# A two-block transformer layer on one Trainium2 core: the first block's front half rebuilt around the gated-delta-net chain

## The chip, the cores and the metric

The kernel runs on one core of a Trainium2 chip. The metric is the device time of one launch in microseconds (us), the median of the runs. The core's engines are PE (TensorE), DVE (VectorE), ACT (ScalarE), POOL (GpSimd) and SP (SyncE, which here only issues transfers).

## The reference

`reference(x, ...)` sends 256 tokens of width 1024 through two blocks. Block 1, the only one that the change touches:

- `mod = silu(c) @ ada_w + ada_b` gives six rows of 1024 (shift, scale and gate for the mixer and for the feed-forward part); `h = rmsnorm(x) * (1 + scale1) + shift1`; `proj = h @ w_in`.
- **The gated delta net (GDN)**, four heads of 128: a causal convolution over four tokens and silu on queries, keys and values, l2 norms on queries and keys, decays `g` and `beta` from the gates, and then chunk by chunk `t_mat = (I + tril(k_beta k^T * decay, -1))^-1`, `u = t_mat (v beta)`, `o = q state + (q k^T * decay) v_new`, an rmsnorm of `o`, times `silu(z)`.
- **The sparse attention (NSA)**, four heads: compressed keys and values (blocks of 32 tokens through a small MLP), selected blocks and a window; with 256 tokens the last two are full causal attention. Three gates weigh the three outputs.
- `x = x + gate1 * (concat(o_gdn, o_nsa) @ w_out)`, and then a convolved gated feed-forward part.

Block 2 (retention, block attention, product-key experts) follows and is the same in both kernels.

## The kernel before

Activations lie transposed, features on the 128 partitions and the 256 tokens along the free axis; `x` is eight such tiles. Weights come from HBM in chunks of 128x1024 f32 (512 KB) by `Core.weights`: SP issues the transfer into one of four `raw` buffers, ACT rounds the chunk to fp32r (`wh`, L165), and DVE or POOL, by the argument `lo`, computes the residual `wl = raw - wh` (L171). Every projection is then three matmuls, `wh*hH`, `wh*hL` and `wl*hH`, since the activations are split in the same way. A matmul on plain f32 operands shows as two instructions in the trace.

Block 1's mixer (`block1_mix`) goes in these steps:

- **Modulation column by column.** `ada_col` (L220) multiplies one chunk of `ada_w` with `csil` (twice silu of `c`, repeated on all partitions) and sums along the free axis: on DVE in one instruction (L229), or as a product on POOL (L226) and a sum on ACT (L227). `h_of(d)` (L443) needs two such columns for each of the eight tiles of `h`, one on each path; 24 more, in `modulation()` (L926), all on POOL and ACT, are needed only at the block's end.
- **F projection.** The contraction is outermost: with each tile of `h`, one chunk of `w1f` (keys and queries) and one of `w1g` (inputs of the compression, and values), and the gates, are multiplied into PSUM (L453 to L466), 14 accumulators and the gates at once, so that all of PSUM is taken. The last two tiles are done together (`f_tail`).
- **Gates and heads.** `sg` and `gl` are sigmoids and log decays; `conv` (L529), `heads` (L549) and `rstd` (L185, ten small DVE instructions that depend on one another) give keys and queries with their inverse norms; key times key is scaled by columns (`rk`) and by rows (`rows` and `gram`, L611 to L630: PE spreads a column over a row, ACT copies it, DVE or POOL multiplies).
- **The inverse.** The two chunks' 128x128 triangles are inverted by doubling (L668 to L690): at each of six levels PE multiplies, DVE masks (L676), PE multiplies again, DVE subtracts (L689). `tt2` holds the inverse and its transpose side by side, and both are updated.
- **Values and output** (L692 to L743), **NSA** (`nsa()`, L797; `proj1` projects keys, queries and `z` by tokens; `scores` and `values` work head by head, and each head's probabilities are scaled by 1/sum on DVE, L900), and **the output projection** `kouter` with `wo1` (L961), whose results are added to `x` on DVE (L958).

These pieces are Python generators (`gdn`, `nsa`, `modulation`, ...), and the loop over `live` (L940 to L951) interleaves them: until the grams are done one step of each per turn, and then two of `gdn`, one of the others, and one of `modulation` every third turn. The tile framework's scheduler then puts the instructions of each engine into an order of its own, and every engine works in that order.

## Time and profile before

| | |
|---|---|
| median of 3 runs | 1553.77 us (1552.84 to 1556.26) |
| profiled execution, its own time | 1555.88 us |
| its span, first to last instruction | 1554.1 us |
| PE busy in the span | 1487.9 us (96%) |
| DVE, ACT, POOL busy | 1085.2, 727.7, 481.1 us |
| instructions | 27243 |

The profiled execution took 1.8 us more than its span, and 2.1 us more than the median. Views are read by stretches of the span: "start us" counts from the first instruction. A granted clock (PEclk) of 1.00 is TensorE's upper level of 2.4 GHz, 0.50 its lower one of 1.2 GHz, and what lies between is a mean over time.

### The profile page before, as it was taken

Reading aid. Unit: us, or ns where it says so; the run is one execution under the profiler, and the core shown is the slowest. Engines: PE = TensorE matmul, PEld = TensorE weight load, DVE = VectorE, ACT = ScalarE, POOL = GpSimd, SP = SyncE. Lnnn points to the kernel's source line nnn. Section 1 sums busy time; section 2 is a strip of 40 time slices with the busy share of each in tenths; the row PEclk is TensorE's granted clock in tenths of the full one; section 3 lists DMA queues with packets and bytes.
Section 4 is the critical chain, followed back from the end, with each engine's and each line's share of the span. In section 5 each row is a group of like instructions: output and inputs, shape, how many; then the busy total and the mean of one; then the engine's idle time right before and its main releaser. Section 6 shows DMA issues by size and latency. Waiting matters only on the chain.

```text
span 1554.1 us, 27243 instructions
## 1 busy us (share of the span) xinstructions
PE 1487.9 (96%) x10805; PEld 1356.2 (87%) x10805; DVE 1085.2 (70%) x2067; ACT 727.7 (47%) x1077; POOL 481.1 (31%) x265
## 2 busy tenths in 40 slices
PE   5889889999999999999999999999999999999998
PEld 4778779999997788999999999999997877788887
DVE  5885786999766477666399953777768788844443
ACT  3453264666544443644544544444444344444443
POOL 4643771332004450012322222222222222232231
PEclk8998899999999999999999999999999999999999
DMA  7753355466675554357555565555556555556664
GB/s 272 236 164 122 122 167 166 145 189 191 216 260 184 168 165 136 109 175 241 168 152 175 174 191 175 168 171 170 169 170 190 154 172 168 176 176 198 182 185 135
DMA packets 77599, 273.82 MB, mean 176 GB/s; under 512 B 9632, under 2 KB 11296, under 8 KB 76832
## 3 DMA queue, kind: packets, MB, share of 16 engines
q1 hardware_dynamic: 74304, 267.06, 55.3%
q10 hardware_dynamic: 3168, 5.03, 1.0%
q8 instruction: 84, 1.38, 0.4%
q14 instruction: 43, 0.35, 0.1%
HBM read 269.96 MB, written 2.10 MB: 175 GB/s over the span
## 4 chain that ended last, share of the span: by engine, by line
PE 80%; DVE 14%; issue 2%; DMA 2%; ACT 1%; POOL 0%; SPq 0%; DVEq 0%; ACTq 0%; POOLq 0%
PE po L306 8%; PE po L307 8%; PE po L308 8%; PE ps_u L296 6%; PE ps_u L298 6%; PE ps_u L297 6%; PE ps_ko L334 4%; PE ps_ko L333 4%; PE ps_ko L335 4%; DVE wl L171 3%; PE ps_mm L307 2%; PE ps_mm L308 2%; PE ps_mm L306 2%; PE ps_up L297 2%; PE ps_up L298 2%
## 5 line engine op out<-in xcount | busy, mean ns | idle before, releaser
L165 ACT ACTIVATE wh<-raw 128x1024 fp32r<-128x1024 f32 (+1 forms) x446 | 468.8, 1053 | 518.9 <-PE ps_u L297 179.0
L171 POOL TENSOR_TENSOR wl<-raw,wh 128x1024 fp32r<-128x1024 f32 (+1 forms) x143 | 354.4, 2480 | 885.7 <-ACT wh L165 837.3
L171 DVE TENSOR_TENSOR wl<-raw,wh 128x1024 fp32r<-128x1024 f32 x303 | 382.2, 1264 | 174.8 <-ACT wh L165 172.3
L298 PE MATMUL ps_u<-hH,wl 128*128 128x256 f32 x1024 | 287.4, 282 | 6.0 <-DVE wl L171 6.0
L296 PE MATMUL ps_u<-hH,wh 128*128 128x256 f32 x1024 | 292.2, 286 | 0.0
L297 PE MATMUL ps_u<-hL,wh 128*128 128x256 f32 x1024 | 288.7, 282 | 0.4 <-DVE hL L171 0.4
L307 PE MATMUL po<-wl,pH 128*128 128x512 f32 x512 | 203.3, 398 | 0.0
L308 PE MATMUL po<-wh,pL 128*128 128x512 f32 x512 | 201.1, 393 | 0.0
L298 PEld LDWEIGHTS ps_u<-hH,wl 128*128 128x128 f32 x1024 | 193.5, 190 | 7.2 <-DVE wl L171 7.2
L297 PEld LDWEIGHTS ps_u<-hL,wh 128*128 128x128 f32 x1024 | 193.9, 189 | 0.6 <-DVE hL L171 0.6
L296 PEld LDWEIGHTS ps_u<-hH,wh 128*128 128x128 f32 x1024 | 193.1, 189 | 0.0
L306 PE MATMUL po<-wh,pH 128*128 128x512 f32 x512 | 167.7, 400 | 0.5 <-ACT A L1348 0.5
L306 PEld LDWEIGHTS po<-wh,pH 128*128 128x128 f32 x512 | 96.3, 188 | 22.1 <-ACT A L1348 0.6
L307 PEld LDWEIGHTS po<-wl,pH 128*128 128x128 f32 x512 | 96.4, 188 | 22.0
L308 PEld LDWEIGHTS po<-wh,pL 128*128 128x128 f32 x512 | 96.2, 188 | 21.7
L171 DVE TENSOR_TENSOR pL<-A,pH 128x512 fp32r<-128x512 f32 x64 | 64.0, 1000 | 57.1 <-ACT pH L165 57.1
L1438 DVE TENSOR_TENSOR oh<-eq,idx 128x512 f16<-128x512 f16 x64 | 29.4, 459 | 80.7 <-PE ps_G L1444 80.7
L165 ACT ACTIVATE pH<-A 128x512 fp32r<-128x512 f32 x64 | 40.3, 631 | 93.6 <-PE po L307 93.5
L307 PE MATMUL ps_mm<-wl,hH 128*128 128x512 f32 x192 | 77.8, 406 | 1.7 <-DVE wl L171 1.7
L298 PE MATMUL ps_up<-nH,wl 128*128 128x256 f32 x272 | 76.2, 280 | 0.8 <-DVE wl L171 0.8
L308 PE MATMUL ps_mm<-wh,hL 128*128 128x512 f32 x192 | 76.6, 400 | 0.0
L297 PE MATMUL ps_up<-nL,wh 128*128 128x256 f32 x272 | 76.1, 280 | 0.0
(498 smaller groups left out, 3246.3 us busy)
## 6 DMA issues: line engine op xcount, KB each, us to landing
raw<-in_pu SPq DMA_DIRECT2D x128, 512.0 KB, 3.7
raw<-in_pvv SPq DMA_DIRECT2D x128, 512.0 KB, 3.7
raw<-in_up SPq DMA_DIRECT2D x44, 512.0 KB, 3.7
raw<-in_w SPq DMA_DIRECT2D x36, 512.0 KB, 3.7
raw<-in_ada SPq DMA_DIRECT2D x32, 512.0 KB, 3.9
raw<-in_down SPq DMA_DIRECT2D x22, 512.0 KB, 4.5
adaw<-in_ada SPq DMA_DIRECT2D x16, 512.0 KB, 4.6
raw<-in_wo SPq DMA_DIRECT2D x16, 512.0 KB, 4.2
```

The lines of the kernel that those rows point to most:

```text
L165: nc.scalar.activation(H, src, AF.Copy)
L171: eng.tensor_tensor(L, src, H.bitcast(F32), ALU.subtract)
L296: nc.tensor.matmul(ps, wH[:, d], xH[:, d], start=d == 0, stop=False)
L297: nc.tensor.matmul(ps, wH[:, d], xL[:, d], start=False, stop=False)
L298: nc.tensor.matmul(ps, wL[:, d], xH[:, d], start=False, stop=d == KD - 1)
L306: nc.tensor.matmul(ps[t], h, a, start=first, stop=False)
L307: nc.tensor.matmul(ps[t], h, b, start=False, stop=False)
L308: nc.tensor.matmul(ps[t], xL[:, d, t * P:(t + 1) * P], a, start=False, stop=last)
L333: nc.tensor.matmul(o, W[0][:, s], xH[:, r], start=r == order[0] and n % 2 == 0, stop=False, skip_group_check=True)
L334: nc.tensor.matmul(o, W[0][:, s], xL[:, r], start=False, stop=False, skip_group_check=True)
L335: nc.tensor.matmul(o, W[1][:, s], xH[:, r], start=False, stop=r == order[-1], skip_group_check=True)
L1438: nc.vector.tensor_tensor(twos(oh), twos(eq), of(2, t0, n), ALU.mult)
```

## The change

It is all in block 1's mixer; from the output projection's weights on, the code and the engines' orders are those of before (their lines are 42 higher).

- **F** now projects queries, keys and gates only (8 accumulators); the values and the inputs of the compression are projected afterwards, feature tile by feature tile (`fproj`, six chunks of `w1g`, residuals on DVE).
- **Norm of x**: squares on ACT, sums on DVE, one short matmul for each half in place of 16 full ones. The row stays in PSUM.
- **Modulation**: all 16 early columns on DVE with a copy of `csil` in PSUM (`csp`); the 24 later ones on DVE too.
- **POOL** keeps three residuals of F and the masks; all others of the mixer are on DVE.
- **Grams**: the scaling by rows is gone. Key grams are scaled by `rk*rk*beta` by columns, values by the inverse (`irk`), queries' norms go into the last rmsnorm.
- **Inverse**: half the columns in the first product; only `T` is updated, and PE transposes it anew at each level with a copy on ACT. Values and queries are prepared after the second level (`inputs`).
- **Compression**: four partial sums in four 32-column groups of PE (`tile_position`), added by a matmul with `sel`.
- **Scalings** of normed keys and queries, probabilities and outputs on ACT.

```diff
@@ norm, modulation, F
+        csp = psa.tile([P, D], F32, name="csp")
+        nc.vector.scalar_tensor_tensor(csp, k.csil, 1.0, crow, ALU.add, ALU.mult)
+        nc.scalar.activation(k.csil, csp, AF.Copy)
...
-                ada_col(k, 2 * d + s, pl.tile([P, WC], F32, tag="tt", bufs=3, name="adaw"), pool=s == 0)
+                w = pl.tile([P, WC], F32, tag="adaw", bufs=3, name="adaw")
+                nc.sync.dma_start(w, I["ada"][2 * d + s])
+                nc.vector.scalar_tensor_tensor(w, w, 0.5, csp, ALU.mult, ALU.mult,
+                                               accum_out=k.mod[:, 2 * d + s:2 * d + s + 1])
...
             h_of(d)
-            f_rows(d, *F0)
-            f_rows(d, *F1)
+            W = k.weights(I["w1f"][d], lo="pool" if d % 2 and d > 2 else "dve")
+            for n in range(8):
+                f_mm(W, n, d)
...
+        first.close()
+        psp = es.enter_context(tc.tile_pool(name="b1ps", bufs=4, space=PSUM))
@@ grams
-                eng.tensor_tensor(g_[:, h, :T], g_[:, h, :T], rw, ALU.mult)
-                eng.tensor_tensor(g_[:, h, T:], g_[:, h, T:], rw[:, P:], ALU.mult)
...
+        nc.vector.scalar_tensor_tensor(irk, pss, 4.0 * EPS, rk, ALU.add, ALU.mult)
+        nc.vector.tensor_tensor(rk, rk, rk, ALU.mult)
+        nc.vector.tensor_tensor(rk, rk, sg[:, :, 0:4], ALU.mult)
@@ inverse
-                    ps = sp([P, 4, P])
+                    ps = sp([P, 4, 64])
                     for h in range(4):
-                        nc.tensor.matmul(ps[:, h], am[c][:, h], tt2[c][:, 0, h], start=True, stop=True)
-                    m1[c] = g512().rearrange("p (a b) -> p a b", b=P)
-                    nc.vector.tensor_tensor(m1[c], ps, lv[:, lvl, None, :].to_broadcast([P, 4, P]), ALU.mult)
+                        nc.tensor.matmul(ps[:, h], am[c][:, h], half(T_[c][:, h:h + 1], b, 0), start=True, stop=True)
...
+                    if lvl > 1:
+                        ps = sp([P, 4, P])
+                        for h in range(4):
+                            nc.tensor.transpose(ps[:, h], T_[c][:, h], k.ident)
+                        nc.scalar.activation(TT[c], ps, AF.Copy)
@@ projections, compression, probabilities
-            ps = yield from proj_T(k, I["w1t"], c, psm, hH, hL, lo="dve" if c == 1 else "pool")
+            ps = yield from proj_T(k, I["w1t"], c, psm, hH, hL, lo="dve")
...
+        def fproj():
+            for n in range(6):
+                if n % 2 == 0:
+                    ps = nq([P, 2, T])
+                mm_F(k, ps[:, n % 2], k.weights(I["w1g"][n]), hH, hL)
+                if n % 2:
+                    nc.scalar.activation(vr[:, n - 3:n - 1] if n > 1 else kcv, ps, AF.Copy)
+                yield
...
-                        nc.tensor.matmul(pcs[i][:15], X[:, 8 * q + l, :15], rv[:, l], start=q == 0 and l == 0,
-                                         stop=q == 3 and l == 7)
+                        j = 32 * (l % 4)
+                        nc.tensor.matmul(pcs[i][j:j + 16], X[:, 8 * q + l], rv[:, l], start=q == 0 and l < 4,
+                                         stop=q == 3 and l >= 4, tile_position=(0, j), skip_group_check=True)
...
-                        nc.vector.tensor_scalar(prs[t][:, b], prs[t][:, b], s4[:, t, b:b + 1], None, ALU.mult)
+                        nc.scalar.activation(prs[t][:, b], prs[t][:, b], AF.Copy, scale=s4[:, t, b:b + 1])
@@ modulation and the loop
-                ada_col(k, n, pool=True)
+                ada_col(k, n)
...
+        def inputs():
+            yield from fproj()
+            while "level 2" not in done:
+                yield
+            yield from vals()
+            yield from queries()
...
         while live:
-            turn += "grams" in done
             for g in list(live):
-                if g is A and turn:
-                    step(g, 2)
-                elif g is not M or (turn and turn % 3 == 0):
-                    step(g)
+                step(g, 2 if g is B else 1)
```

Three places of the engines' orders. First PE, behind the end of F, in the kernel before (L466 writes F's last accumulators, L558 the sums of squares of the keys' heads, L813 the compression's sums):

```order
L466 MATMUL sp<-hH,wl 128x256
L558 MATMUL sp<-ones,sq 128x1 x2
L813 MATMUL nq<-raw,t_920 15x128 x11
L558 MATMUL sp<-ones,sq 128x1 x2
L813 MATMUL nq<-raw,t_920 15x128 x7
L558 MATMUL sp<-ones,sq 128x1 x2
L813 MATMUL nq<-raw,t_920 15x128 x4
L558 MATMUL sp<-ones,sq 128x1 x2
L813 MATMUL nq<-raw,t_920 15x128 x10
L813 MATMUL nq<-raw,t_963 15x128 x32
```

And in the change, past the middle of `fproj` (L299 to L301; L845 is the compression, L568 the sums of squares):

```order
L299 MATMUL nq<-hH,wh 128x256
L845 MATMUL nq<-raw,t_812 16x128 x6
L568 MATMUL sp<-ones,sq 128x1 x4
L845 MATMUL nq<-raw,t_812 16x128 x2
L300 MATMUL nq<-hL,wh 128x256
L301 MATMUL nq<-hH,wl 128x256
```

The compression stood alone on PE behind F; it now stands in eleven pieces among the 144 matmuls of `fproj`, which were part of F.

Second POOL in the middle of the mixer, before (`am` is the first masked triangle, `qa` the query grams, `raw<-raw,csil` a column of the modulation):

```order
L658 TENSOR_TENSOR am<-ga,lv 128x512 x2
L171 TENSOR_TENSOR wl<-raw,wh 128x1024
L226 TENSOR_TENSOR raw<-raw,csil 128x1024 x3
L171 TENSOR_TENSOR wl<-raw,wh 128x1024 x2
L226 TENSOR_TENSOR raw<-raw,csil 128x1024
L629 TENSOR_TENSOR qa<-qa,rows 128x256
L630 TENSOR_TENSOR qa<-qa,rows 128x128
```

And POOL in the change, from F's third residual to the residuals of the feed-forward part:

```order
L503 TENSOR_SCALAR cneg<-cmask 128x128
L836 TENSOR_TENSOR t_812<-kcv,posT 128x32x15
L836 TENSOR_TENSOR t_993<-kcv,posT 128x32x15
L637 AFFINE_SELECT dec<-dec 128x2x128 x4
L850 MEMSET t_1094 128x128
L860 MEMSET t_1106 128x128
L171 TENSOR_TENSOR wl<-raw,wh 128x1024 x21
```

All work of POOL between the decays' masks and the feed-forward part has moved away.

Third DVE at the fourth and fifth level of the inverse, before (L676 masks, L689 subtracts; the others are NSA's softmax):

```order
L676 TENSOR_TENSOR g_1576<-sp,lv 128x512
L855 TENSOR_TENSOR sc<-nq,cneg 128x128
L857 TENSOR_REDUCE mx<-sc 128x8
L858 TENSOR_TENSOR sc<-sc,mx 128x128
L676 TENSOR_TENSOR g_1589<-sp,lv 128x512
L860 TENSOR_REDUCE mx<-sc 128x8
L689 TENSOR_TENSOR tt<-tt,sp 128x16x16 x2
```

And in the change (L680 masks, L697 subtracts, L232 is a column of the modulation):

```order
L680 TENSOR_TENSOR g_1854<-sp,lv 128x256
L697 TENSOR_TENSOR T<-T,sp 128x16x16
L171 TENSOR_TENSOR wl<-raw,wh 128x1024 x2
L232 SCALAR_TENSOR_TENSOR raw,mod<-raw,csil 128x1024
L171 TENSOR_TENSOR wl<-raw,wh 128x1024
L697 TENSOR_TENSOR T<-T,sp 128x16x16
L232 SCALAR_TENSOR_TENSOR raw,mod<-raw,csil 128x1024
L680 TENSOR_TENSOR g_1941<-sp,lv 128x256
L171 TENSOR_TENSOR wl<-raw,wh 128x1024
L680 TENSOR_TENSOR g_1957<-sp,lv 128x256
```

Between the chain's steps there now stand the wide instructions that were POOL's, and NSA's softmax has moved behind the inverse.

## Rows read from the trace of the kernel before

**Rows 1.** Stretches of the span by stage: busy time of each engine, granted clock, DMA
```profile
0.00:26.05 26.05, 7.04 (x36) 6.59 (x36) 14.15 (x26) 8.58 (x13) 11.91 (x17) 0.84 0.83 294
26.05:82.50 56.45, 48.49 (x363) 46.13 (x364) 47.50 (x69) 27.27 (x49) 32.63 (x18) 0.92 0.69 222
82.50:125.33 42.83, 37.88 (x265) 32.29 (x264) 34.49 (x98) 21.32 (x52) 15.71 (x14) 1.00 0.53 163
125.33:241.06 115.73, 103.07 (x593) 91.68 (x592) 82.27 (x167) 53.69 (x137) 70.40 (x36) 0.84 0.45 146
241.06:264.10 23.04, 23.04 (x195) 22.74 (x194) 14.81 (x32) 9.33 (x11) 1.75 (x1) 1.00 0.52 161
264.10:1554.10 1290.00, 1268.41 (x9362) 1156.79 (x9360) 891.98 (x1679) 607.50 (x818) 348.67 (x181) 1.00 0.57 175
```

**Rows 2.** Timeline of DVE: start, duration, line, operation, tiles, what ended a wait
```profile
9.17 1.23 DVE L397 SCALAR_TENSOR_TENSOR csil<-csil,crow 128x1024 f32<-128x1024 f32 x1 [9.17 <-ACT csil L371]
...
52.59 3.42 DVE L171 TENSOR_TENSOR wl<-raw,wh 128x1024 fp32r<-128x1024 f32 x1
...
61.57 1.22 DVE L229 SCALAR_TENSOR_TENSOR adaw<-adaw,csil 128x1024 f32<-128x1024 f32 x1
...
63.10 0.16 DVE L448 TENSOR_TENSOR md<-md,c_norms 128x1 f32<-128x1 f32 x1
63.28 1.23 DVE L171 TENSOR_TENSOR wl<-raw,wh 128x1024 fp32r<-128x1024 f32 x1
...
264.10 1.69 DVE L958 SCALAR_TENSOR_TENSOR x<-ps_ko,mod,x 128x256 f32<-128x256 f32 x4 [3.40 <-PE ps_ko L335]
```

**Rows 3.** Timeline of POOL in the same stretch of F
```profile
52.34 2.59 POOL L226 TENSOR_TENSOR adaw<-adaw,csil 128x1024 f32<-128x1024 f32 x1
54.89 2.81 POOL L171 TENSOR_TENSOR wl<-raw,wh 128x768 fp32r<-128x768 f32 x1
```

**Rows 4.** DVE by line and shape, 125 to 241 us: busy us, mean ns, idle before
```profile
L900 DVE TENSOR_SCALAR pr<-pr,s 128x256 f32<-128x256 f32 x8 | 8.7, 1128 | 0.1
L689 DVE TENSOR_TENSOR tt<-tt,sp 128x256 f32<-128x256 f32 x22 | 8.2, 412 | 6.2 <-PE sp L686 6.1
L676 DVE TENSOR_TENSOR g<-sp,lv 128x512 f32<-128x512 f32 x12 | 8.2, 682 | 0.8 <-PE sp L674 0.7
```

**Rows 5.** POOL by line and shape, 73 to 262 us
```profile
L226 POOL TENSOR_TENSOR raw<-raw,csil 128x1024 f32<-128x1024 f32 x24 | 56.6, 2373 | 23.8 <-DMA raw<-in_ada 13.2 <-DVE tt L663 6.2 <-ACT pr L890 3.0
```

**Rows 6.** Timeline of PE at F's end, twelve matmuls in a row: first and last
```profile
76.00 0.28 PE L464 MATMUL ps_f<-hH,wh 128*128 128x256 f32 x1
...
77.29 0.28 PE L464 MATMUL sp<-hH,wh 128*128 128x256 f32 x1
```

**Rows 7.** PE by line and shape, 82.5 to 125.3 us
```profile
L813 PE MATMUL nq<-raw,t 128*15 128x128 f32 x128 | 14.7, 273 | 0.1
```

**Rows 8.** Timeline of PE: one product of the inverse, and one tiled product
```profile
170.21 1.92 PE L674 MATMUL sp<-tt,ga 128*128 128x128 f32 x8
...
186.59 1.11 PE L674 MATMUL sp<-tt,ga 128*128 128x128 f32 x8
...
206.84 0.48 PE L910 MATMUL nq<-pcT,vcm 16*128 16x128 f32 x2
207.25 1.16 PE L914 MATMUL nq<-pT,vv 128*128 128x128 f32 x8
```

**Rows 9.** Two more stretches: busy DVE is the third engine's number
```profile
180.00:220.00 40.00, 38.62 (x254) 33.34 (x254) 33.93 (x73) 22.74 (x60) 33.22 (x15) 1.00 0.54 182
...
280.00:330.00 50.00, 46.53 (x383) 45.69 (x382) 48.89 (x84) 34.57 (x73) 18.97 (x8) 1.00 0.53 159
```

**Rows 10.** Waits, 0 to 320 us: total us, number, longest
```profile
POOL raw L226 <- DMA raw<-in_ada: 13.2, 6, 9.4
```

**Rows 11.** DMA issues: number, KB each, us to landing
```profile
raw<-in_ada SPq DMA_DIRECT2D x32, 512.0 KB, 3.9
```

**Rows 12.** ACT by line and shape, 125 to 241 us
```profile
L227 ACT ACTIVATE raw<-raw 128x1024 f32<-128x1024 f32 x24 | 25.1, 1046 | 2.1 <-POOL raw L226 2.1
```

More of the change, by code (lines that the diff above doesn't have):

```diff
@@ L225, in ada_col @@
     if pool:
-        nc.gpsimd.tensor_tensor(raw, raw, k.csil, ALU.mult)
+        for q in range(0, WC, WC // pool):
+            v = raw[:, q:q + WC // pool]
+            nc.gpsimd.tensor_tensor(v, v, k.csil[:, q:q + WC // pool], ALU.mult)
         nc.scalar.activation(raw, raw, AF.Copy, scale=0.5, accum_out=k.mod[:, n:n + 1])
@@ L379, in block1_mix @@
         psm = es.enter_context(tc.tile_pool(name="b1pm", bufs=4, space=PSUM))
-        psp = es.enter_context(tc.tile_pool(name="b1ps", bufs=4, space=PSUM))
+        first = es.enter_context(ExitStack())
+        psa = first.enter_context(tc.tile_pool(name="b1pa", bufs=1, space=PSUM))
         k.sm = sm
@@ L583, in block1_mix @@
         pv = k.c1["pv"]
+        gq1 = pl.tile([P, 1], F32, name="gq1")
+        nc.vector.tensor_scalar(gq1, pv[:, 1:2], P ** -0.5, None, ALU.mult)
         def g512():
@@ L687, in gdn @@
-                    for i in both:
-                        tv = half(tt[:, i], b, i)
-                        nc.vector.tensor_tensor(tv, tv, ps[:, i].rearrange("p h (n b) -> p h n b", b=b), ALU.subtract)
+                            nc.tensor.matmul(ps[:, h], TT[c][:, h], m1[c][:, h], start=True, stop=True)
+                        else:
+                            nc.tensor.matmul(ps[:64, h], m1[c][:, h], TT[c][:, h, 64:], start=True, stop=True)
+                    if lvl < 6:
+                        tv = half(T_[c], b, 0)
+                        nc.vector.tensor_tensor(tv, tv, ps.rearrange(split, b=b), ALU.subtract)
+                    else:
+                        tv = TT[c][:64, :, 64:]
+                        nc.vector.tensor_tensor(tv, tv, ps[:64], ALU.subtract)
@@ L763, in proj1 @@
             for t in range(NT):
-                nc.vector.tensor_tensor(raw[t][:, :n], pr[t][:, :n], r[:, t, :, None].to_broadcast([P, n, P]), ALU.mult)
+                for i in range(n):
+                    nc.scalar.activation(raw[t][:, i], pr[t][:, i], AF.Copy, scale=r[:, t, i:i + 1])
             for i in range(n):
@@ L800, in nsa @@
             vcm = pl.tile([P, P], F32, name="vcm")
+            sel = pl.tile([P, 16], F32, name="sel")
+            nc.vector.tensor_reduce(sel, k.ident.rearrange("p (a b) -> p b a", b=32)[:, :16], AX.X, ALU.add)
             pcs = []
@@ L842, in nsa @@
             yield from proj1(1)
-            live.extend((gate(), vals()))
-            mix.append(pl.tile([P, KD, T], F32R, tag="yk", name="mH"))
+            live.append(gate())
+            mix.append(pl.tile([P, KD, T], F32R, name="mH"))
             mix.append(pl.tile([P, KD, T], F32R, name="mL"))
@@ L853, in nsa @@
             nc.gpsimd.memset(pc, 0.0)
[L854 removed]
+            sc = low.rearrange("p (t h n) -> p t h n", t=NT, h=4)
             nc.vector.tensor_tensor(sc, psc, cneg, ALU.add)
```

211 lines of the change are left out of this document (106 added, 105 removed).

## The prediction

> **What bounds the kernel now.** I read the busy time by stretches first [rows 1]. Only block 1's mixer differs, and the engines' orders are the same from the output projection on; so the reader should cut the span where the first result of that projection is added to `x`, at 264.10 us [rows 2]. The 1290.0 us behind it, in which PE is busy 1268.4, are taken over unchanged. The forecast is the time at which this addition starts in the new kernel, and nothing else.
>
> Ahead of it there are five stretches: 26 us until F begins, 56.5 us of F, 42.8 us to the inverse, 115.7 us of inverse, projections and attention, and 23.0 us of output projection [rows 1]. PE is never the full bound there: it is idle 8 us in F, 5 in the third stretch, 12.7 in the fourth, and the granted clock is 0.92 and 0.84 in F and the fourth, a mix of the two levels (2.4 and 1.2 GHz) with PE's idle gaps ahead of the lower one. One product of the inverse takes 1.11 us where the clock is up and 1.92 where it is down [rows 8].
>
> Next, what the gaps wait for. A residual on DVE takes 1.23 us alone and 3.42 us when POOL works through two products beside it [rows 2, 3]; instructions with two operands in SBUF come to a standstill there. A DVE instruction that reads PSUM doesn't: L676 kept 682 ns, L689 412 ns, over a stretch in which POOL was busy 70.4 of 115.7 us, whereas the scaling L900 took 1128 ns for the same 256 elements [rows 1, 4]. So POOL's help lengthens DVE's chain, and DVE's chain is what PE waits for.
>
> **The change, part by part.**
>
> *Start.* The product with `c` starts at 9.17 us [rows 2]; it hangs on the same transfer and the same ACT instruction as before, so I keep it. The norm's 16 matmuls go; two short ones and ACT squares replace them, and the first matmul of F still needs the same row, so nothing is gained before 26 us. The sums of squares are in the DVE count that follows.
>
> *F.* DVE's order, from that product to the last tile of `h`, holds 16 column sums (1.22 us each: 19.5), 6 residuals (1.2: 7.2), one other 1024-wide instruction (1.2), 3 of 512 (0.68: 2.0), 17 of 256 (0.41: 7.0), 3 of 128 (0.3, an estimate between 0.41 and 0.16: 0.9) and 28 small ones (0.16: 4.5) [rows 2, 4]: 42.3 us, so 51.5. POOL keeps three residuals. The column sums read `csp` in PSUM, which lets them pass; the others can be held by up to 2.4 us each time, 0 to 7.2 in all. I take half, 3.6. Behind the last tile, ACT's rounding (0.5) and the 48 matmuls of the last two tiles at 0.117 us (12 of them start within 1.29 us [rows 6]) make 6.1. **F ends at 61.2 us** instead of 82.5. Transfers: 24 chunks of 512 KB replace 24 plus 8 smaller ones; before, 222 to 294 GB/s were moved [rows 1], and 12.6 MB at 294 take 43 us; they begin ahead of DVE's 42.3 us of work, which hides them. I cost them at nothing; at 222 they take 57 us and would end F some 9 us later, which stays in the range.
>
> *To the inverse.* Now PE is the bound. `fproj` is 144 matmuls of 0.117: 16.8. The compression's 128 instructions took 14.7 us [rows 7]. It is tiled in the change, and its price isn't in the trace: the only tiled product there, L910, needed 0.41 us for two instructions until the next began [rows 8], no quicker than plain ones. Bounds: a quarter of 14.7 plus 0.2 for each of eleven visits (5.9), and 14.7 plus the same 2.2 (16.9). I take 14.7, the value nearest L910. What else PE did in the third stretch: 37.9 busy, less 14.7, less 48 matmuls of 512 columns that now come later (twice 0.117 each: 11.2), less 16 instructions for spreading rows that vanish (1.8): 10.2 stays. Masking the triangles, now two 512-wide DVE instructions: 1.4. Together 43.1: **the inverse starts at 104.3 us** (before: 125.3). DVE has 31 us of work in this time and keeps up; ACT loses POOL's column sums and has room.
>
> The Trainium skill, "TensorEngine Tiling (Array Packing)", section Key Properties, says that different tiles load and multiply in parallel, but also that changing the tiling mode drains TensorE. By its first half the compression would take 5.9 us and the forecast would be 9 us lower; by its second half and L910, it is the 14.7 to 16.9 above. The rival below carries it.
>
> *Inverse to output projection.* Here DVE gets what POOL had: 22 of the 24 column sums fall here. On POOL they took 56.6 us [rows 5]. DVE's order from the masking to the last head's residual holds 22 sums (26.8), 14 residuals ahead of the output projection's last five (16.8), 13 instructions of 512 (8.8), 55 of 256 (22.6), 26 of 128 (7.8) and 95 small ones (15.2): 98.0 us. PE has about as much (three token projections 33.7, the inverse 232 instructions at 0.14 or less [rows 8], the attention, all at the upper clock) and fits beside it; ACT loses the 24 sums (25.1 [rows 12]) and gets 16 probability scalings and some 40 shorter copies in their stead. So DVE is the bound, and the question is how dense it runs. In the busiest 40 us of the old stage, with the clock up, it was busy 33.93 (85%), with POOL beside it; at the start of the feed-forward part 48.89 of 50 (98%) [rows 9]. I take 90%, nearer the first since the chain is the same: 109 us, from 102.9 to **211.8**.
>
> *Output projection.* Until the first addition it needs 156 matmuls (18.3 us) and the last head's remainder, some 2: before, the stretch was 23.04 with more of the attention in it [rows 1]. **The first addition starts at 232.3 us.**
>
> *Sum.* 264.1 - 232.3 = 31.8 us gained: 21.3 in F, nothing more to the inverse (it now contains `fproj`), 10.5 after it. The profiled execution took 1555.88 us, 2.1 more than the median shown, 1553.77; the same gain on the median gives **1522 us**.
>
> **Rivals.**
>
> *The tiled compression runs its column groups side by side.* For: the four groups write disjoint partitions, and the 64 products are ordered group after group. Against: L910, and eleven switches between tiled and plain products. It lies on PE's path to the inverse, so 14.7 becomes 5.9: **1513 us**. Chance 0.22.
>
> *DVE waits as much as before.* In the old fourth stretch it was busy 82.27 of 115.73, 71% [rows 1]. The inverse's steps depend on one another through PE, and in the new order wide instructions stand between its masks and subtractions; each may hold the next step by 1.2 us. Against: part of those waits came from POOL, and values, queries and projections now fill PE. 98.0 at 71% is 138 us instead of 109: 29 of the 31.8 us are gone, **1551 us**. Chance 0.13.
>
> *Slower: DVE stands still for transfers.* All chunks share four `raw` buffers and one queue in order. POOL waited 13.2 us, six times, for columns of `ada_w` [rows 10], and nobody cared; DVE now takes them in order with the chain behind it. A landing takes 3.9 us [rows 11]. If 8 of the 24 sums wait for a whole landing (31.8/3.9), the gain is gone; if half of them do, 47 us are lost: **1569 us**. For: one such wait on POOL lasted 9.4 us. Against: only six in 24 waited, and the queue moved 146 GB/s where 294 have been seen. Chance 0.05.
>
> *The clock.* If PE has more gaps in the inverse, its 232 instructions cost up to 24 us more at the lower level (0.81 us for eight [rows 8]), as they partly did before; this is inside the second rival's price and gets no chance of its own.
>
> *The change doesn't take POOL out of the chain.* The order speaks against it: behind F, POOL has only masks and the windows' additions. What remains beside DVE, three residuals in F, is priced. Chance 0.02, at about no change.
>
> **How the numbers follow.** The forecast has 0.58. Its own range: 98% instead of 90% on DVE is 9 us less and no collision in F another 3.6 less (1509); 80% is 13.5 more, full collision 3.6, late transfers 9 (1548, if all come together). Adding the compression at its quick end and the nearer half of the 71% case, **1505 to 1546** leaves about 0.08 below and 0.12 above. A difference of 0.2% (3 us) is what a measurement of this kernel can tell. Faster: 0.58 + 0.22 and most of the second rival's 0.13, 0.92; the same: the rest of it, the last rival and a little of the third, 0.04; slower: 0.04.
>
> **What would show it.** In the new profile: F's last matmul near 61 us; residuals on DVE at 1.2 us throughout, and none above 2 behind F; the first masked triangle at 103, the inverse at 104; DVE busy about 90% from there to 212 with column sums between the level's steps; the first addition near 232 us; and 1290 us behind it. The tiled compression shows itself at once: 64 products in 6 or in 15 us of PE's time. I am wrong on the first step if F ends past 66 or before 57; on the third if DVE is busy under 80% or the chain's longest waits name a transfer; and on everything if what lies behind the first addition changes by more than 3 us.

## The result and the profile after

The changed kernel is 1.0% slower: 1567.78 us median (six runs, 1566.32 to 1573.1) against 1553.3 us for the kernel before (six runs); the ratio is 1.010, 95% interval 1.0076 to 1.0123. The forecast was 1522 us, and its range ended at 1546. The profiled execution took 1567.32 us with a span of 1565.6 us, so the same cut as before the change can be made, at the first addition to `x`.

Stretches of the span of the changed kernel (length, busy time and count of PE, PEld, DVE, ACT, POOL, granted clock, DMA share, GB/s). In order: up to F's first matmul; F; from F's end to the inverse's first product; the inverse; from the first masked triangle to the last head's residual (99.91 to 256.90, for which the prediction took 109 us); what lies behind the first addition; 20 us around the start of the inverse; and everything from F's end to the first addition:

```profile
0.00:28.10 28.10, 2.18 (x8) 1.86 (x8) 16.34 (x41) 9.79 (x15) 2.90 (x17) 1.00 0.92 329
28.10:63.05 34.95, 29.62 (x217) 28.16 (x218) 27.62 (x51) 12.25 (x19) 8.55 (x8) 0.95 0.71 241
63.05:108.54 45.49, 36.14 (x342) 30.98 (x343) 38.41 (x100) 23.55 (x54) 5.38 (x8) 0.88 0.65 209
108.54:190.69 82.15, 73.80 (x385) 65.61 (x385) 52.09 (x131) 24.42 (x64) 0.00 (x0) 0.75 0.52 164
99.91:256.90 156.99, 130.72 (x632) 110.78 (x633) 87.68 (x249) 58.56 (x156) 0.20 (x1) 0.73 0.39 125
...
276.69:1565.60 1288.91, 1266.51 (x9362) 1154.88 (x9360) 891.21 (x1679) 606.96 (x818) 348.94 (x181) 1.00 0.57 175
100.00:120.00 20.00, 10.93 (x45) 9.59 (x46) 18.20 (x44) 5.70 (x14) 0.20 (x1) 0.50 0.56 163
63.05:276.69 213.64, 183.74 (x1123) 159.62 (x1124) 123.51 (x337) 86.02 (x212) 7.25 (x9) 0.79 0.44 141
```

Against [rows 1]: behind the first addition nothing changed (1288.91 us for 1290.0). F ends at 63.05 instead of 82.5, so 19.5 us are gained there. Then all of it is lost, and more: from F's end to the first addition the changed kernel takes 213.64 us, where the kernel before takes 181.5.

The same stretch in the kernel before:

```profile
82.60:264.10 181.50, 163.90 (x1048) 146.61 (x1047) 131.48 (x295) 84.24 (x198) 87.76 (x51) 0.90 0.48 152
```

Of the 32.1 us, PE's busy time is 19.8 (183.74 less 163.90) and its idle time 12.3 (29.9 less 17.6). The instruction counts differ by 7%, but busy time multiplied by granted clock is nearly the same: 183.74 x 0.79 is 145, 163.90 x 0.90 is 148. So PE did about as much, longer, at a lower mean clock. In the runs below that product comes to 143 to 149, once 139 (the two with extra matmuls left aside), which makes this reading a rough yardstick: what a version loses is PE's idle time, plus PE's busy time above some 146 us.

Where it begins is in the timeline of PE of the changed kernel, from the end of the compression on (start, duration, line, operation, tiles, what ended the idle time before):

```profile
95.88 0.40 PE L854 MATMUL nq<-sel,t 128*128 128x16 f32 x2
100.65 2.11 PE L662 MATMUL sp<-ident,am 128*128 128x128 f32 x8 [4.37 <-DVE am L659]
105.21 0.80 PE L863 MATMUL nq<-c,t 128*128 128x128 f32 x2 [2.45 <-DVE t L861]
108.54 3.68 PE L677 MATMUL sp<-T,ga 128*128 128x64 f32 x16 [2.53 <-DVE T L665]
114.18 3.68 PE L692 MATMUL sp<-g,TT 128*128 128x64 f32 x16 [1.96 <-DVE g L680]
119.33 1.97 PE L677 MATMUL sp<-T,ga 128*128 128x64 f32 x8 [1.47 <-DVE T L697]
...
129.70 0.47 PE L309 MATMUL ps_mm<-wh,hH 128*128 128x512 f32 x1
```

From 96 to 125 us PE has only the chain and the compression's small network (L854, L863), and it waits for DVE at nearly each step; the granted clock of 100 to 120 us is 0.50, which is the lower of its two levels (1.2 of 2.4 GHz). The first matmul of the token projections, the wide work that doesn't hang on the chain, comes at 129.70. What DVE does meanwhile is in its timeline:

```profile
117.65 1.23 DVE L232 SCALAR_TENSOR_TENSOR raw<-raw,csil 128x1024 f32<-128x1024 f32 x1 [1.73 <-DMA raw<-in_ada]
...
118.87 0.40 DVE L697 TENSOR_TENSOR T<-T,sp 128x256 f32<-128x256 f32 x1
...
119.64 0.40 DVE L697 TENSOR_TENSOR T<-T,sp 128x256 f32<-128x256 f32 x1
...
121.33 0.43 DVE L680 TENSOR_TENSOR g<-sp,lv 128x256 f32<-128x256 f32 x1 [0.49 <-PE sp L677]
```

A column sum (L232) waits 1.73 us for its transfer, takes 1.23, and only then come the subtractions (L697) for which PE's product at 119.33 waited. All column sums and all residuals of weights in the stretch from F's end to the first addition, by line and shape (busy us, mean ns, idle before):

```profile
L171 DVE TENSOR_TENSOR wl<-raw,wh 128x1024 fp32r<-128x1024 f32 x25 | 30.4, 1221 | 33.7 <-ACT wh L165 33.5
L232 DVE SCALAR_TENSOR_TENSOR raw<-raw,csil 128x1024 f32<-128x1024 f32 x24 | 29.4, 1226 | 15.8 <-DMA raw<-in_ada 13.2 <-PE sp L634 2.4
```

Residuals and sums run at their undisturbed 1.22 us: POOL is out of the way, as meant. But 18 of the 24 sums stand between the inverse's steps (22.0 us inside 108.54 to 190.69).

### The profile page after: what moved, and what is told of

Same layout as the page of the kernel before. It is cut to its first block, busy times and chain, and to the rows that moved or that the text cites. A ratio compares the mean times of both kernels' runs of the same rounds, so it can differ in the third digit from the quotient of the medians.

```text
span 1565.6 us, 26969 instructions
## 1 busy us (share of the span) xinstructions
PE 1482.0 (95%) x10707; PEld 1344.5 (86%) x10707; DVE 1058.7 (68%) x2105; ACT 715.0 (46%) x1062; POOL 367.6 (23%) x214
## 4 chain that ended last, share of the span: by engine, by line
PE 77%; DVE 15%; DMA 4%; issue 2%; ACT 2%; ACTq 0%; DVEq 0%
PE po L309 8%; PE po L310 8%; PE po L311 8%; PE ps_u L299 7%; PE ps_u L301 6%; PE ps_u L300 6%; PE ps_ko L337 4%; PE ps_ko L336 4%; PE ps_ko L338 4%; DVE wl L171 4%; DMA raw<-in_ada 2%; PE ps_mm L310 2%; PE ps_mm L309 2%; PE ps_mm L311 2%; PE ps_G L1485 1%
## 5 line engine op out<-in xcount | busy, mean ns | idle before, releaser
L165 ACT ACTIVATE wh<-raw 128x1024 fp32r<-128x1024 f32 x444 | 468.6, 1057 | 515.4 <-PE ps_u L300 181.8
L171 POOL TENSOR_TENSOR wl<-raw,wh 128x1024 fp32r<-128x1024 f32 x130 | 325.7, 2507 | 996.8 <-ACT wh L165 945.1
L171 DVE TENSOR_TENSOR wl<-raw,wh 128x1024 fp32r<-128x1024 f32 x314 | 391.2, 1248 | 197.6 <-ACT wh L165 196.2
L301 PE MATMUL ps_u<-hH,wl 128*128 128x256 f32 x1024 | 287.5, 282 | 6.0 <-DVE wl L171 6.0
L299 PE MATMUL ps_u<-hH,wh 128*128 128x256 f32 x1024 | 292.1, 286 | 0.0
L311 PE MATMUL po<-wh,pL 128*128 128x512 f32 x512 | 201.1, 393 | 0.0
L301 PEld LDWEIGHTS ps_u<-hH,wl 128*128 128x128 f32 x1024 | 193.5, 190 | 7.2 <-DVE wl L171 7.2
L299 PEld LDWEIGHTS ps_u<-hH,wh 128*128 128x128 f32 x1024 | 193.1, 189 | 0.0
L309 PE MATMUL po<-wh,pH 128*128 128x512 f32 x512 | 167.7, 400 | 0.5 <-ACT A L1390 0.5
L309 PEld LDWEIGHTS po<-wh,pH 128*128 128x128 f32 x512 | 96.3, 188 | 22.2 <-ACT A L1390 0.6
L311 PEld LDWEIGHTS po<-wh,pL 128*128 128x128 f32 x512 | 96.2, 188 | 21.7
L301 PE MATMUL ps_up<-nH,wl 128*128 128x256 f32 x272 | 76.0, 280 | 0.8 <-DVE wl L171 0.8
L311 PE MATMUL ps_mm<-wh,hL 128*128 128x512 f32 x192 | 76.7, 401 | 0.0
L299 PE MATMUL ps_up<-nH,wh 128*128 128x256 f32 x272 | 75.8, 279 | 0.0
```

What stands on the lines that cost most here:

```text
L165: nc.scalar.activation(H, src, AF.Copy)
L171: eng.tensor_tensor(L, src, H.bitcast(F32), ALU.subtract)
L299: nc.tensor.matmul(ps, wH[:, d], xH[:, d], start=d == 0, stop=False)
L301: nc.tensor.matmul(ps, wL[:, d], xH[:, d], start=False, stop=d == KD - 1)
L309: nc.tensor.matmul(ps[t], h, a, start=first, stop=False)
L311: nc.tensor.matmul(ps[t], xL[:, d, t * P:(t + 1) * P], a, start=False, stop=last)
```

## The experiments

The theories, by the letters in the expectations. On the 24 sums: **A** and **T**, late transfers of the columns in DVE's order; **B** and **D**, the sums' own DVE time (DVE is the bound; in e18's expectation D is worded as S is here); **C**, they use DVE's idle time and the loss is elsewhere; **Q**, their place in the one queue, ahead of the projections' weights; **R**, a column in the shared buffers costs wherever it stands; **S**, sums between the inverse's levels delay the chain. On PE: **K**, its gaps keep it at the lower level; **P**, its independent work comes too late behind the compression's network. Each stretch quoted below is F's end to the first addition, columns as above; the scheduler reorders other instructions with each edit, so whole orders are compared.

### What do the 24 columns cost?

e1 takes them out (columns 16 to 39 of `mod` become zeros):

```
-   ada_col(k, n)
+   if n == 16: nc.gpsimd.memset(k.mod[:, 16:40], 0.0)
```

> The changed kernel without the 24 later modulation columns: neither their transfers nor their sums (the 24 values are set to 0, so gate, shift and scale of the output projection and the feed-forward part are wrong). Theory A (DVE stands still in its order for columns that land late): the first addition to x comes at 235 to 245 us instead of 276.7, the time is 1526 to 1536 us. Theory B (the sums' own 29 us stand in DVE's order ahead of the inverse's steps): the same, 1530 to 1540. Theory C (the sums lie in DVE's idle time; the attention comes last, one head after the other, behind the inverse): within 6 us of the changed kernel, 1562 to 1568.

e2 keeps the sums and drops the transfers (sums over `csil`, so those columns are wrong values):

```
-   ada_col(k, n)
+   w = pl.tile([P, WC], F32, tag="adaw", bufs=3, name="adaw")
+   nc.vector.scalar_tensor_tensor(w, k.csil, 0.5, k.csil, ALU.mult, ALU.mult, accum_out=k.mod[:, n:n+1])
```

> The changed kernel with its 24 later column sums on DVE, but taken over a tile that lies in SBUF all the time (csil twice), so that the columns' transfers are left out and the values are wrong. Theory A (late transfers): nearly all of what the kernel without sums gains, 1528 to 1540 us, and DVE dense between the inverse's steps. Theory B (the sums' own time): no more than the 13.2 us of direct waits for columns come back, 1553 to 1562. Theory C: 1562 to 1568, as without sums.

e3 gives the columns the three `adaw` buffers instead of the shared ones; e4 keeps the shared ones but gives the columns back to POOL and ACT:

```
+   e3: ada_col(k, n, pl.tile([P, WC], F32, tag="adaw", bufs=3, name="adaw"))
+   e4: ada_col(k, n, pool=1)
```

> The changed kernel with three buffers of their own for the 24 later columns (those of the early columns, idle by then) instead of the four that they share with the weights. Theory A in the form that the shared buffers hold the transfers up: DVE's waits for columns (13.2 us, 10 times) and ACT's for weights shrink to under 5 us, and the time falls by 8 to 20 us, to 1548 to 1560. If the one queue in order and the landing time of 4 to 5 us decide, not the buffers: less than 4 us of difference. Theories B and C: less than 4 us too.

> The changed kernel with the 24 later columns where they were before: the product on POOL, the sum on ACT. Theory A and B: DVE's order is free of them, nothing in the chain waits for a column; some DVE instructions with two SBUF operands stand still beside POOL (24 products of 2.4 us, each holding one of them up by 1 to 2 us where they meet, 10 to 20 us in all), so 1540 to 1555 us. Theory C: no change from moving them, but the collisions come on top, 1565 to 1580.

Measured: e1 1526.54 us (0.982 of before, 0.977 to 0.988), e2 1542.89 (0.993, 0.990 to 0.996), e3 1535.62 (0.990, 0.984 to 0.995), e4 1563.38 (1.007, 1.004 to 1.010). Without the columns the change is worth 27 us; with them it costs 14, so the columns cost 41 us. C falls, and e1 can't tell A from B. e2, e3 and e4 lie outside every range that was named for them, and e2 and e3 don't say why the columns are dear, since the order moved: in e2 sums went into F (which ended at 73.6), in e3 all 24 stood ahead of the inverse, whose first product came at 138.7. Both are nevertheless quicker than the change. In e4 DVE's 29.4 us of sums are gone, yet it is as busy (125.7 us), because other instructions were stretched beside POOL's products. DVE by line and shape of e4 shows it:

```profile
L545 DVE SCALAR_TENSOR_TENSOR t<-yk,gconv,t 128x253 f32<-128x253 f32 x4 | 3.8, 976 | 0.0
L545 DVE SCALAR_TENSOR_TENSOR t<-vr,gconv,t 128x253 f32<-128x253 f32 x4 | 3.6, 913 | 0.0
...
L923 DVE TENSOR_SCALAR m<-m 128x4 f32<-128x4 f32 x4 | 3.3, 834 | 0.1
```

The first of them takes 470 ns in the changed kernel, the second 472, the third 164. The Trainium skill, "SBUF — State Buffer", section "Who interferes with whom", says that a DVE instruction with two SBUF inputs contends with a GpSimd instruction that reads SBUF; the two rows of L545 agree. They are the smaller part, though: most of the stretching fell on small instructions of the dependent chains (the steps of `rstd`, the softmax), some of which, as L923, have one tensor operand.

### Is it the pace, the queue or the buffers?

e5 steps the columns in every third turn after the grams; e10 makes one ring of seven buffers; e14 issues all 24 ahead of the loop; e11 is the kernel before with a column in every turn:

```
+   e5:  turn += "grams" in done
+        if g is not M or (turn and turn % 3 == 0): step(g, 2 if g is B else 1)
+   e10: tag="raw", bufs=7 (columns, weights and the early columns)
+   e14: step(M, 6)                  # in each of the four turns ahead of the loop
+   e11: (turn and turn % 3 == 0)  ->  turn      # in the kernel before
```

> The changed kernel, shared buffers, with a later column only every third turn and only once the key grams are done, as in the kernel before; nothing else. On the queue 8 of the 12 chunks of the token projections' weights then stand ahead of all columns but one, and the last 2 behind 4 columns instead of 14. Theory Q (on the one queue with its four shared buffers the columns stand ahead of the token projections' weights, so the attention's inputs come late): the first addition at 240 to 255 us, the time 1530 to 1545. Theory R (a column in the shared buffers costs the same wherever it stands in the queue): 1555 to 1568. Theory S (the gain with buffers of their own came from the sums standing ahead of the inverse in DVE's order): 1560 or more, since they don't here.

> The changed kernel with one ring of seven shared buffers in place of four shared and three for the early columns. Same memory, same order of code. Theory Q in the form that buffers decide (a column that waits to be summed keeps a buffer from the weights): about what own buffers gave, 1530 to 1545. Theory Q in the form that the place in the queue decides: the columns still stand ahead of the weights, 1555 to 1566. Theory S: 1560 or more, since most sums still stand between the inverse's levels.

> The changed kernel, shared buffers, sums on DVE, all 24 later columns taken ahead of the inverse (six in each of the four turns before the loop); nothing else. Theory S (sums and their waits between the inverse's levels cost the time, not the buffers): DVE does them in one stretch, PE idles once and then runs the inverse and the attention closely packed at the upper clock, as with own buffers: the first addition at 240 to 252 us, 1530 to 1545 us. Theory Q or R (buffers or place in the queue): the weights of values and of the compression now stand behind 18 to 24 columns, which is the worst case: 1570 or more.

> The kernel before with a later column on every turn once the grams are done instead of every third; the sums stay on POOL and ACT. On the queue the last 4 of the 12 chunks for the token projections stand behind 7 to 10 columns instead of 2 to 4. Theory Q: slower than the kernel before by 5 to 20 us. Theories R and S: within 4 us of the kernel before, as the columns, their buffers and DVE's order of sums are the same.

Measured: e5 1562.16 us (1.007, 1.004 to 1.009), e10 1563.68 (1.007, 1.004 to 1.010), e14 1561.56 (1.008, 1.005 to 1.011), e11 1548.54 (0.999, 0.997 to 1.001). Pace and the number of buffers are worth 4 to 6 us of the 41 (e5, e10). e11 speaks against Q: the kernel before took 1551.0 us beside it, and no loss came. e14 met no forecast: S had 1530 to 1545 us for it, Q and R 1570 or more. In it 20 sums stand ahead of the inverse's first product (117.7), and it gains little; a likely reason is in SP's timeline (start, duration, line, tiles, number of issues):

```profile
105.73 9.34 SPq L225 DMA_DIRECT2D raw<-in_ada  x6
116.48 6.56 SPq L840 DMA_DIRECT2D raw<-in_cv  x4
123.18 51.05 SPq L158 DMA_DIRECT2D raw<-in_w1t  x12
```

The projections' weights are issued only behind the columns, from 123.18 on, in the same four buffers; in the changed kernel the first is issued at 93.16. So with shared buffers the sums can be early or the weights can, not both.

### Sums ahead of the chain, or between its steps

What differs by intent is the place. All have the convolutions of values held behind the inverse's second level. e7 gives the columns their own buffers; although the program steps them from level 1 on, the scheduler takes most of them ahead of the inverse, since nothing holds them; e9 also lets each transfer start only behind a subtraction of the inverse, so all 24 sums stand between its steps; e18 is e9 with the sums over `csil`, without transfers; e8 holds the convolutions alone, in the change's shared buffers.

```
+   nc.vector.scalar_tensor_tensor(gv, held[0][:, 0, :32], 0.0, gv, ALU.mult, ALU.add)   # all four: hold
+   ada_col(k, n, <adaw tile>); M stepped from "level 1" on                              # e7
+   nc.vector.tensor_copy(mk, T_[c][:, 0, :1])      # e9, e18: mark behind a subtraction
+   nc.gpsimd.tensor_copy(w[:, :1], marks[-1])      # e9, e18: ahead of each column
```

> The changed kernel with own buffers for the columns, and the convolutions of values and queries not before the second level (their coefficients are written anew from a result of the first). Most of the sums stand ahead of the inverse, 15 us of convolutions between its levels. Theory S: the inverse's first product 10 to 15 us earlier than at 138.7 with own buffers alone, and since the convolutions need no transfer the chain behind it is only a little slower: 1522 to 1536. Theory D or K in the form that any wide work between the levels opens PE's gaps: most of the gain is lost again, 1545 to 1562.

> The changed kernel with shared buffers and sums as they are, but the convolutions of values and queries not before the inverse's second level. Theory P: 15 us of DVE's work leave the place ahead of the compression's network, the projections start 8 to 15 us earlier than 129.7 and the time falls by 5 to 20 us, 1546 to 1561. Theory D: the wide work between the levels grows, 1565 to 1580.

> The changed kernel with the columns' own three buffers, but each column's transfer may start only after a step of the inverse (a mark that DVE writes behind the subtractions), so that the sums stand between the levels; the convolutions of values and queries can't start before the second level either (their coefficients are written anew from a result of the first). Theory Q: the weights pass the columns, so no slower than with own buffers alone, and the inverse's first product comes at 95 to 105 us instead of 138.7 there: 1515 to 1535. Theory S: with the sums between the levels again, the chain is as slow as in the changed kernel: 1550 to 1568.

> The kernel with gated columns (own buffers, sums between the inverse's levels, convolutions held), but each sum taken over csil twice, which lies in SBUF: the 24 columns' transfers are left out, and the values are wrong. In the kernel with the transfers DVE waited 8.2 us for columns. Theory T (waits for the transfers in DVE's order make the place between the levels dear): 1524 to 1540 us, near the kernel with the sums ahead of the inverse (1523.9). Theory D (1.2 us of DVE between two dependent steps is dear by itself, wherever the data lie): 1548 to 1560, no more than the 8.2 us back.

Measured: e7 **1523.87 us** (0.982, 0.978 to 0.986), e8 1568.17 (1.010, 1.007 to 1.013), e9 1559.36 (1.004, 1.002 to 1.006), e18 1560.56 (1.006, 1.003 to 1.008). The stretch in e7, then its part ahead of the inverse, the inverse, and the rest:

```profile
65.74:232.02 166.28, 154.58 (x1123) 136.67 (x1124) 121.63 (x331) 85.16 (x212) 10.00 (x9) 0.95 0.47 164
65.74:119.63 53.89, 46.81 (x394) 40.41 (x395) 52.13 (x124) 23.70 (x51) 8.14 (x8) 0.97 0.90 323
119.63:184.38 64.75, 60.21 (x391) 53.21 (x390) 45.04 (x144) 35.60 (x107) 0.00 (x0) 0.89 0.23 78
184.38:232.02 47.64, 47.56 (x342) 43.05 (x341) 24.46 (x65) 25.85 (x55) 1.86 (x1) 1.00 0.32 100
```

The same stretch, the inverse and the rest in e9:

```profile
63.63:263.76 200.13, 175.93 (x1123) 154.57 (x1124) 124.49 (x347) 86.57 (x212) 14.26 (x33) 0.84 0.46 150
97.72:185.47 87.75, 72.41 (x381) 65.06 (x382) 72.50 (x185) 33.12 (x83) 7.96 (x26) 0.77 0.68 228
185.47:263.76 78.29, 70.05 (x404) 59.87 (x404) 28.83 (x96) 37.28 (x94) 1.86 (x1) 0.85 0.19 61
```

DVE by line and shape, the sums ahead of the inverse in e7:

```profile
L232 DVE SCALAR_TENSOR_TENSOR adaw<-adaw,csil 128x1024 f32<-128x1024 f32 x18 | 23.0, 1283 | 0.5 <-DMA adaw<-in_ada 0.4
```

And the sums inside the inverse in e9:

```profile
L232 DVE SCALAR_TENSOR_TENSOR adaw<-adaw,csil 128x1024 f32<-128x1024 f32 x24 | 29.3, 1220 | 8.3 <-DMA adaw<-in_ada 8.2
```

DVE has about the same work in both (121.63 and 124.49 us), and so has PE by the yardstick above (147 and 148). e7 starts its inverse 22 us later, with DVE at 97% ahead of it, and yet has its inverse done at 184.38 where e9 needs until 185.47. So the chain isn't done later in e9; what is lost lies behind it. There PE has 47.6 us left in e7, at the full clock and without a gap, for e9's 78.3 us. Of these 30.7 us, 8.2 are idle time of PE, 10.5 the lower clock and 11.9 more work left over (70.05 x 0.85 is 59.5, against 47.6), the projections among it: 30 matmuls of L309 to L311 for 48. The idle time is nearly all attention, whose products wait for ACT's probabilities, as e9's waits from 185.47 to 263.76 say (total us, number, longest):

```profile
PE nq L946 <- ACT pr L942: 7.9, 2, 4.2
```

The place, with what the scheduler moves along with it, is worth 35 us by the medians. In the two profiled executions 31.7 us of their difference lie ahead of the first addition and 7.0 behind it, where the code is the same. And e18, where the 24 transfers are gone, is no quicker than e9:

```profile
63.20:271.04 207.84, 174.88 (x1124) 152.05 (x1124) 123.50 (x347) 86.52 (x212) 23.54 (x33) 0.83 0.27 84
```

So A, T, Q and R fall as the main cause, and so do B and D as an amount of work, since DVE's work is equal. S stands as far as the place goes; how it delays the rest is more than the chain alone, as the 30.7 us show. Two reservations: e9 and e18 carry small marks and POOL copies that e7 doesn't, and e18's DVE waited 12.6 us for ACT's rounding of weights instead of e9's 2.4, so "transfers cost nothing" holds for the total, not for each wait. e8 shows that holding the convolutions does nothing while the sums stay where they were.

### Is it PE's clock, or its order?

e12 fills PE's gaps in the change with 224 unread matmuls of 256 columns (26.2 us at the 0.117 us of F's end [rows 6]); e13 does it in e9:

```
+   fill(ps, n): n x nc.tensor.matmul(ps[:, 256:], hH[:, 0, :P], hH[:, 0, :T], start=True, stop=True)
+   24 ahead of each of two first transposes, 6 per product, 8 per head
```

> The changed kernel with matmuls that nobody reads put into PE's order where it waits: 24 of 256 columns ahead of each of the two first transposes, 6 ahead of each product of the inverse, 8 ahead of each head's output, 224 in all, 26 us at the upper clock. Theory K (the gaps cost little by themselves, but keep PE at its lower clock, where the same work takes 33 us longer): the granted clock between 111 and 257 us rises from 0.75 to 0.9 or more, and the time falls to 1540 to 1558 in spite of the added work. Theory D (DVE's order is the bound, and PE's clock only follows): the clock rises too, but the time stays within 5 us of 1566 or grows by up to 20.

> The same 224 unread matmuls in the kernel with gated columns (own buffers, sums and convolutions between the levels). Theory K: faster than without them, 1530 to 1550 instead of 1559. Theory D: 1555 to 1580.

Measured: e12 1566.92 us (1.012, 1.006 to 1.018), e13 1570.67 (1.013, 1.008 to 1.017). The stretch in e12:

```profile
64.47:272.83 208.36, 192.73 (x1348) 173.19 (x1348) 123.76 (x336) 85.93 (x212) 7.48 (x9) 0.91 0.45 144
```

The clock rose from 0.79 to 0.91. If the filler is taken at its 26.2 us (an estimate), PE's other busy time is 166.5 us instead of 183.7, and its idle time 15.6 instead of 29.9: 31.5 us gained, 26.2 paid for the filler; nothing measurable in the kernel's time is left. Both times lie in D's ranges and outside K's, and e13 is 11 us slower than e9. So the part of K that filled gaps raise the granted clock is shown; that the clock by itself sets the time is not.

e15 puts the first token projection ahead of the compression's network; e17 does it in e7:

```
+   nc.scalar.activation(pcT[j:j + 16, i], pcs[i][j:j + 16], AF.Copy)   # both banks copied at once
+   yield from proj1(0)
    for i, n in enumerate("kv"):
...
-   yield from proj1(0)
    yield from proj1(1)
```

> The changed kernel, its columns, buffers and convolutions as they are; only the first token projection (16 of the 48 passes of three matmuls, and the transposes behind it) stands ahead of the compression's small network instead of behind it (the compression's four partial sums are copied to SBUF at once, so their PSUM banks come free). Theory P (PE's independent work comes too late: it waits for the compression's small network, whose DVE steps stand among sums, residuals and convolutions, so PE is idle ahead of the inverse, has gaps in it, and does the last projection and the attention behind it): the projection starts at 97 to 103 us instead of 129.7, the first addition comes at 245 to 262, the time is 1535 to 1553. Theory D (sums and transfer waits between the levels set the time): 1558 to 1568.

> Own buffers for the columns, convolutions of values and queries not before the second level, and the first token projection ahead of the compression's network: the kernel that took 1523.9 us, with the projection moved. Theory P: the projections start 5 to 10 us earlier than at 106.5, 1510 to 1522. Theory D: no difference of over 3 us from 1524.

Measured: e15 1553.49 us (1.002, 0.999 to 1.004), e17 1541.76 (0.995, 0.992 to 0.997). In the change it gives 14 us, about as P forecast: the projections start at 97.99. In e7, where P forecast a gain, the same edit costs 18: the compressed values, which attention needs, are ready at 155.18 instead of 108.38. So P is a part of the cause in the change, and no rule.

### Is POOL better out?

e19 gives the residuals of two of the three token projections back to POOL in the change, e20 in e7:

```
-   lo="dve"
+   lo="dve" if c == 1 else "pool"
```

> The changed kernel with the residuals of the first and the last token projection (8 of 1.22 us) on POOL again, as before; POOL does nothing else in that stretch. Theory D (DVE's one order is where the chain's steps, the sums and the residuals stand in each other's way): 9.8 us leave that order, at most 8 collisions of 1 to 2 us come in: 3 to 10 us faster than the changed kernel, 1557 to 1564. If only the sums matter, or if PE's gaps have another cause: within 3 us of 1567, or slower by the 2.4 us that POOL needs for a residual.

> The same 8 residuals on POOL in the kernel with own buffers and held convolutions (1523.9 us), whose DVE is 97% busy ahead of the inverse. Theory D: the inverse's first product 2 to 6 us earlier than at 119.6, and 1517 to 1523. If POOL's products hold up the sums beside them, which have both operands in SBUF: 1525 to 1540.

Measured: e19 1571.31 us (1.011, 1.004 to 1.019), e20 1534.14 (0.987, 0.981 to 0.992). Neither is quicker than the version it was made from (D had forecast 3 to 10 us for e19), so taking POOL off these residuals lost nothing.

**The best version is e7**, 1523.87 us, quicker than the kernel before and than the change.

## Why the prediction was wrong

- *Start and what lies behind the first addition.* Right in the main: no gain came, F's first matmul even stood at 28.10 instead of 26.05; and 1288.91 us for 1290.0 behind the first addition.
- *F.* The time was right, 63.05 for 61.2 and inside the 57 to 66 named, in part by errors that cancel. From the product with `c` to the last tile of `h` (8.70 to 58.76) the changed kernel has:

```profile
8.70:58.76 50.06, 27.50 (x189) 25.88 (x190) 43.67 (x89) 15.99 (x22) 8.80 (x9) 0.97 0.86 302
```

  DVE's 43.67 us are near the 42.3 counted, but they hold the collisions: beside POOL's three residuals two small DVE instructions of L464 took 1.67 and 0.95 us instead of 0.15, and one of L289 2.62 instead of 0.47, 4.5 us in all for the 3.6 taken. DVE's idle 6.4 us stood in no term, and the end behind the last tile took 4.3 us for 6.1.
- *To the inverse.* The start was missed by 4.2 us (108.54 for 104.3), out of errors with opposite signs, besides F's end, which came 1.9 late. The compression's 128 instructions took not 14.7 us but 6.4, so the first rival's term was right and the nearest row, L910 [rows 8], misled. And "DVE keeps up" failed: PE waited 4.37, 2.45 and 2.53 us for it ahead of the first product. The first masked triangle came at 99.91, ahead of the 102.9 forecast, but the inverse's first product only 8.6 us behind it, where the masking's 1.4 us were all that the sum had. What the quick compression gave was spent waiting.
- *Inverse to output projection: the step that failed.* "So DVE is the bound, and the question is how dense it runs." The prediction took 90%, 109 us. It took 157.0 us (99.91 to 256.90), in which DVE was busy 87.68 us, 56%. The count of 98.0 was near; the model was wrong. DVE isn't a bound that a density describes: it is shared by a chain that goes to and fro between PE and DVE and by 24 sums that hang on nothing, in one order. Where the sums stood decided, as e7 and e9 show with about equal amounts of work. The counting also passed over where PE's own work stood: 48 matmuls of the projections were left until behind the inverse, and none came ahead of it, where the kernel before had 48 there; so PE had little to do beside the chain's first steps.
- *The clock.* It was given "no chance of its own" and priced on 232 instructions of the inverse. It bore on the whole stretch: busy time of PE 183.74 us at 0.79, where e7 has 154.58 at 0.95. Of the 47.4 us by which that stretch is longer than e7's, 29.2 are PE's busy time and 18.2 its gaps. That gaps stand ahead of the lower level had been read from [rows 1] and wasn't carried into the sum.
- *The rivals.* The second had the mechanism ("each may hold the next step by 1.2 us") and took old 71% as its worst case; 56% is what came. It should have been worked out as a delay per step with PE's answer at the lower level, not as another density. The third gave 1569 us, next to what was measured, by luck: DVE did wait for columns, 13.2 us in ten times and not a whole landing for twelve sums, and in e9's order, where it waited 8.2 us, nothing is gained without the transfers (e18).
- *POOL out of the chain.* Right: the weights' residuals behind F took 1.22 us each. Giving POOL work again helped little or nothing: e4 is 4 us quicker than the change, e19 and e20 are no quicker than what they were made from.
- *The output projection.* Right: 19.8 us (256.90 to 276.69) for 20.5.

Shown: the columns cost 41 us (e1), and some 35 us hang on their place and on what moves with it (e7 against e9), not on transfers (e18, in e9's order). Open: why 29.4 us of sums cost more than their own time. PE's lower clock beside its gaps is large enough to account for it, but e12 couldn't separate the two, since filling costs about what it gives.

## What to carry to other kernels

An engine that takes its instructions in order can't be priced by its amount of work and a density: write down which wide, independent instructions stand between two steps of a dependent chain, and what the other engine of the chain has to do meanwhile. In this kernel such work was cheap in a stretch in which the waiting engine had other work, although the chain then started later (e7 against e9: 22 us later, and done 1 us earlier). For that, what it read needed buffers of its own; in shared ones it pushed the next weights back (e14).

## Unexpected of the hardware

- The product in four column groups, with eleven visits between plain matmuls, as PE by line and shape of the changed kernel has it:

```profile
L845 PE MATMUL nq<-raw,t 128*16 128x128 f32 x128 | 6.4, 276 | 0.0
```

  Before, 128 instructions of 273 ns took 14.7 us [rows 7]; now they take 276 ns each and 6.4 us together, so they ran side by side. The Trainium skill, "TensorEngine Tiling (Array Packing)", section Key Properties, says that different tiles load and multiply in parallel: the row agrees. It also says that a change of the tiling mode drains TensorE. The 6.4 us are 2.7 more than a quarter of 14.7, an estimate of some 0.25 us for each of the eleven visits; what of it is a drain, no run here shows.
- Beside POOL's products of 2.5 us, convolutions with two operands in SBUF went from about 470 to means of 976 and 913 ns, and a scaling of 128x4 elements (L923) from 164 to 834 ns, while the weights' residuals kept 1221 ns in the same stretch of e4; so POOL's cost fell on whichever instructions stood beside it and can't be read from one form.
- Ahead of and inside the 20 us at a granted clock of 0.50 PE had idle gaps of 4.37, 2.45, 2.53, 1.96 and 1.47 us; with gaps filled, the mean clock from F's end to the first addition went from 0.79 to 0.91 (e12), without a gain in time.
